# Attention scores of the last two layers from split float32r pairs, two heads in turn, with the mask added on VectorE

## The chip, the cores and the metric

The kernel runs on one core of a Trainium2 chip. The metric is device time in microseconds, the median of several runs; one further execution is profiled. The engines are TensorE (PE in the profile, its weight loads PEld), VectorE (DVE), ScalarE (ACT), GpSimd (POOL) and SyncE (SP), which issues the DMAs of the weights.

## The reference

Four layers over 256 tokens of width 1024. The first two (an mLSTM and differential attention layer, a convolution and mixture-of-experts layer) aren't touched. The last two are alike; what they compute, cut to the attention:

```
u = x * (1 + scale) + shift;  h = u @ w_in             # q, k, v of three attentions, gates
dsa: 4 heads of 64, one shared k and v; each query sees its 64 best keys by an index score
fox: 6 heads of 64; s = q k^T / 8 + cum[t] - cum[s]; causal
nsa: 6 heads of 64 in 2 groups; compressed blocks (16 keys), selected keys (ks, vs), window (kw, vw)
     o = g0 * o_cmp + g1 * o_slc + g2 * o_win          # with 256 tokens slc and win are causal
p = softmax(s with mask);  o = p @ v
y = (concat(dsa, fox, nsa) * silu(gate)) @ w_out;  x = layer_norm(ALPHA * x + (1 + gate2) * y)
```

## The kernel before

All tokens fit in two blocks of 128 (`tb`). Weights come in chunks of 1 MB over SP's queue (`Stream`, L164) and are split into a float32r part `hi` by ScalarE (L98) and a rest `lo` by VectorE or, for each third half chunk, GpSimd (L99); a product is then three float32r matmuls (`mm3`, L92 to L94). The instructions of each engine are put in order ahead of time by a planner that knows costs, so matmuls of projections stand between those of attention heads.

Each of the last two layers (`Hybrid`) runs in the order of `run`: `p_dsa`, `p_nsa` and `p_cmp` project queries, keys and values (`tok` gives tokens on partitions, tile `ht`; `feat` gives features on partitions, tile `hf`). `rope` rotates (L1477 to L1481), and `to_feat` transposes on TensorE into the one `hx` bank (L1490) and copies out by `copy`, on ScalarE and VectorE in turn (L1448, L1450). `dsa_select` finds each query's 64 best keys on VectorE (L1743 to L1753) and leaves a bfloat16 mask `sel`. Then come the heads: `nsa` (12 calls of `attn` a layer), `p_fox`, `dsa` (4), `nsa_cmp`, two `p_gates`, `fox` (6), two more `p_gates`, `gated`, and `out`.

`attn` does one head in one PSUM bank (tag `at`, five of them). For each token block it adds the mask by a bfloat16 matmul with the identity (L1703), then the float32 scores (L1704; 64 rows, 128 or 256 columns; a float32 matmul shows as two passes, each with a weight load), and for `fox` the decay by a float32r matmul over `cum` (L1707). VectorE takes the maximum (L1709), ScalarE the exponential and its sum (L1711), TensorE transposes the three blocks (L1714), `copy` brings them to SBUF, and three matmuls multiply by v (L1717 to L1719); VectorE scales (L1720 to L1723). Queries, keys and gates: `dqT`, `dkT`, `fqT`, `fkT`, `nrT`, `ksT`, `kwT`, in float32, where head h lies on partitions 0 to 63 if h is even and 64 to 127 if it is odd. `nrT`, `ksT`, `kwT` and `vs` lie in `hgt`, the tile of the gates, and are shown under that name.

Of the kernel before, what the change touches and what calls it, by code (L numbers as in the profile page):

```python
# [21 lines left out]
T = 256  # L22
# [1369 lines left out]
class HybConst:  # L1392


    def __init__(self, e, I, sb):
# [20 lines left out]
        self.causal = (e.neg_ge, e.neg_ge)  # L1416
# [6 lines left out]
class Hybrid:  # L1423
    def __init__(self, e, st, U, I, l, K, mix, sb, wk, ps):
# [3 lines left out]
        t = lambda n, *s, dt=F32: sb.tile([128, *s], dt, name=n)  # L1428
        self.mix = mix
        self.dqT, self.dkT, self.dv = t("hdqT", 2, T), t("hdkT", T), t("hdv", 2, 64)  # L1430
        self.iqT, self.ikT, self.iw = t("hiqT", 2, T), t("hikT", T), t("hiw", 2, 8)
        self.fkT, self.fv = t("hfkT", 3, T), t("hfv", 2, 384)
        self.fqT, self.nqT, self.vw = t("hfqT", 3, T), t("hnqT", 3, T), t("hvw", 2, 128)

        g = t("hgt", 8 * T)
        self.gt = g.rearrange("p (b n) -> p b n", b=2)
        v = lambda i, n, m: g[:, T * i:T * (i + n)].rearrange("p (a t) -> p a t", t=m)
        self.nrT, self.ksT, self.kwT, self.vs = v(0, 3, T), v(3, 2, T), v(5, 2, T), v(7, 1, 128)
# [44 lines left out]
    def to_feat(self, x, out):  # L1483

        e = self.e
        n = out.shape[1]
        p = self.bank("hx", "hx").rearrange("p (a t) -> p a t", a=2)
        for i in range(n):
            for tb in range(2):
                e.nc.tensor.transpose(p[:, i, 128 * tb:128 * tb + 128], x[:, tb, 128 * i:128 * i + 128], e.ident)  # L1490
        self.copy(out, p[:, :n, :])
# [11 lines left out]
    def p_dsa(self, bf):  # L1503
# [12 lines left out]
        self.to_feat(a, self.dkT[:, None, :])  # L1516
# [42 lines left out]
    def p_nsa_q(self, p, j, n):  # L1559
# [4 lines left out]
        self.to_feat(a, self.nrT[:, j:j + n // 128, :])  # L1564

    def p_fox(self):
        e, nc = self.e, self.e.nc
        for i in range(3):
            w = self.st.next()
            for f in range(2):  # L1570
                p = self.feat(w, f)
                j = 2 * i + f
                if j < 3:
                    nc.scalar.activation(self.fqT[:, j, :], p, AF.Copy, scale=0.125)
                else:
                    self.copy(self.fkT[:, j - 3, :], p)
# [58 lines left out]
    def p_nsa_kv(self):  # L1635
        nc = self.e.nc
        for kT, v in ((self.ksT, self.vs), (self.kwT, self.vw)):
# [5 lines left out]
            self.to_feat(a[:, :, 0:128], kT[:, 0:1, :])  # L1643
            self.to_feat(a[:, :, 64:192], kT[:, 1:2, :])
            nc.gpsimd.tensor_copy(v, b[:, :, 128:256])

    def p_gates(self, i):
# [3 lines left out]
        t = self.gt[:, :, 256 * i:256 * i + 256]  # L1651
# [3 lines left out]
    def gated(self, mT, i):  # L1655
# [4 lines left out]
        nc.vector.scalar_tensor_tensor(m, m, 0.5, self.gt[:, :, cs], op0=OP.mult, op1=OP.mult)  # L1660
# [4 lines left out]
        hi, lo = (x[:, 2 * i:2 * i + 2, :] for x in mT)  # L1665
# [3 lines left out]
    def run(self, bf, pe, mT, later):  # L1669
# [4 lines left out]
        self.nsa(range(3))  # L1674
        self.cmp()
        self.nsa(range(3, 6))
# [5 lines left out]
        self.fox((4, 5, 0, 1, 2, 3))  # L1682
        for i in OUT[2:]:
            self.p_gates(i)
        for i in OUT:
            self.gated(mT, i)


    def attn(self, qT, kT, v, masks, out, extra=None, gate=None):
# [5 lines left out]
        s = self.bank("as", "at")  # L1695
        o = s[:, 384:512].rearrange("p (b d) -> p b d", b=2)
        z = wk.tile([128, 2], F32, tag="az", name="az", bufs=4)
        m = wk.tile([128, 2], F32, tag="am", name="am", bufs=4)
        x = wk.tile([128, 384], F32, tag="ax", name="ax", bufs=2)
        parts = [s[:, 0:128], s[:, 128:384]]  # L1700
        for tb, st in enumerate(parts):
            n = 128 * tb + 128
            nc.tensor.matmul(st[:, n - masks[tb].shape[-1]:], e.identb, masks[tb], start=True, stop=False, skip_group_check=True)  # L1703
            nc.tensor.matmul(st, qT[:, 128 * tb:128 * tb + 128], kT[:, 0:n], start=False, stop=(extra is None),  # L1704
                             skip_group_check=True)
            if extra is not None:
                nc.tensor.matmul(st, extra[0], extra[1][:, 0:n], start=False, stop=True, skip_group_check=True)  # L1707
# [594 lines left out]
```

## Time and profile before

| | us |
|---|---|
| median of 3 runs (2023.22 to 2026.17) | 2023.52 |
| profiled execution | 2031.13 |
| its span | 2029.4 |
| mean granted TensorE clock, of 1 | 0.933 |

A median is compared with a median; durations come from the profiled execution, 2031.13 us, of which 1.7 us lie outside the span.

### The profile page before, as it was taken

The numbers are of one execution on the slowest core, as the hardware profiler recorded it, in microseconds if no ns is written. First come the engines' busy times: TensorE is split into PE (matmuls) and PEld (weight loads), VectorE is DVE, ScalarE is ACT, GpSimd is POOL, SyncE is SP. The second block draws the span as 40 slices with busy tenths as digits, with TensorE's granted clock in tenths as the row PEclk, the third lists the DMA queues.
The fourth block names the chain that finished last, engine by engine and source line by source line (L and its number), as shares of the span: only waits on it lengthen the run. The fifth ranks groups of instructions, "written<-read, shape, count | busy, mean of one in ns | idle before, by whom it ended". The sixth has DMA issues, their size and how long they took to land. (4 is left out here: it accounts for less than half of the span.)

```text
span 2029.4 us, 33102 instructions
## 1 busy us (share of the span) xinstructions
PE 1873.0 (92%) x12339; PEld 1657.9 (82%) x12339; DVE 1582.0 (78%) x2239; ACT 1189.8 (59%) x1838; POOL 517.9 (26%) x460
## 2 busy tenths in 40 slices
PE   6789889699997779999999999999997899989997
PEld 3768667699976668999999999999996888878886
DVE  5887996677669758999999999999996674568455
ACT  5455564455545447777777777777776443454333
POOL 2645662533227531000000000000001523333141
PEclk8889987799998889999999999999998988988889
DMA  9845775288753128999999999999993431233120
GB/s 361 285 154 208 244 242 178 80 323 308 250 208 127 50 83 322 366 342 338 346 365 351 333 354 358 342 342 355 355 355 115 135 105 63 89 130 111 65 72 21
DMA packets 132462, 468.41 MB, mean 231 GB/s; under 512 B 14994, under 2 KB 16274, under 8 KB 132292
## 3 DMA queue, kind: packets, MB, share of 16 engines
q1 hardware_dynamic: 131008, 464.38, 64.2%
q8 instruction: 99, 1.62, 0.3%
q10 hardware_dynamic: 1172, 1.65, 0.2%
q14 instruction: 71, 0.58, 0.1%
q0 software_dynamic: 112, 0.17, 0.1%
HBM read 465.10 MB, written 1.05 MB: 230 GB/s over the span
## 5 line engine op out<-in xcount | busy, mean ns | idle before, releaser
L99 DVE TENSOR_TENSOR lo<-raw,hi 128x1024 fp32r<-128x1024 f32 x678 | 858.1, 1280 | 134.9 <-ACT hi L98 112.3
L98 ACT CAST hi<-raw 128x1024 fp32r<-128x1024 f32 x718 | 747.1, 1050 | 300.4 <-PE ph L94 92.8
L93 PE MATMUL ph<-lo,gh 128*128 128x256 f32 x1408 | 397.0, 282 | 3.6 <-DVE lo L99 1.8
L94 PE MATMUL ph<-hi,gl 128*128 128x256 f32 x1408 | 396.7, 282 | 0.0
L92 PE MATMUL ph<-hi,gh 128*128 128x256 f32 x1408 | 394.0, 280 | 0.0
L93 PEld LDWEIGHTS ph<-lo,gh 128*128 128x128 f32 x1408 | 264.6, 188 | 12.6 <-DVE lo L99 6.9
L94 PEld LDWEIGHTS ph<-hi,gl 128*128 128x128 f32 x1408 | 264.8, 188 | 3.4
L92 PEld LDWEIGHTS ph<-hi,gh 128*128 128x128 f32 x1408 | 264.8, 188 | 2.8
L343 POOL TENSOR_TENSOR adac<-adac,raw 128x512 f32<-128x512 f32 x112 | 194.0, 1757 | 180.1 <-ACT raw L341 109.0
L1597 POOL MEMSET kv<- 64x2 f32 x4 | 0.4, 97 | 791.8 <-DVE lo L99 775.1
L99 POOL TENSOR_TENSOR lo<-raw,hi 128x1024 fp32r<-128x1024 f32 (+1 forms) x40 | 97.5, 2446 | 186.9 <-ACT hi L98 178.5
L93 PE MATMUL pe<-lo,hhi 128*128 128x512 f32 x352 | 138.0, 393 | 0.0
L92 PE MATMUL pe<-hi,hhi 128*128 128x512 f32 x352 | 137.2, 397 | 0.5 <-ACT hhi L98 0.5
L94 PE MATMUL pe<-hi,hlo 128*128 128x512 f32 x352 | 125.8, 392 | 0.0
L92 PE MATMUL ht<-hi,Hh 128*128 128x256 f32 (+1 forms) x384 | 117.8, 307 | 0.6 <-ACT u L459 0.6
L93 PE MATMUL ht<-lo,Hh 128*128 128x256 f32 (+1 forms) x384 | 116.0, 302 | 0.0
L94 PE MATMUL ht<-hi,Hl 128*128 128x256 f32 (+1 forms) x384 | 115.8, 302 | 0.0
L92 PE MATMUL ph<-Fh,hi 128*128 128x256 f32 x352 | 101.5, 290 | 11.4 <-DVE h L980 8.8
L93 PE MATMUL ph<-Fl,hi 128*128 128x256 f32 x352 | 101.4, 289 | 0.0
L94 PE MATMUL ph<-Fh,lo 128*128 128x256 f32 x352 | 100.2, 287 | 0.0
L92 PEld LDWEIGHTS ht<-hi,Hh 128*128 128x128 f32 x384 | 79.6, 207 | 2.3 <-ACT u L459 1.4
L1083 POOL TENSOR_TENSOR cyp<-cyp,ctp 128x256 f32<-128x256 f32 x83 | 72.4, 883 | 34.8 <-ACT ctp L1082 31.2
(592 smaller groups left out, 4124.3 us busy)
## 6 DMA issues: line engine op xcount, KB each, us to landing
raw<-in_l_moe_w SPq DMA_DIRECT2D x528, 512.0 KB, 5.3
raw<-in_l_mod_w SPq DMA_DIRECT2D x96, 512.0 KB, 5.4
raw<-in_l_ffn_w SPq DMA_DIRECT2D x66, 512.0 KB, 4.9
raw<-in_w_in SPq DMA_DIRECT2D x60, 512.0 KB, 3.5
raw<-in_w_ada SPq DMA_DIRECT2D x32, 512.0 KB, 5.4
raw<-in_l_w_in SPq DMA_DIRECT2D x28, 512.0 KB, 5.6
raw<-in_l_conv_pw_w SPq DMA_DIRECT2D x24, 512.0 KB, 4.3
raw<-in_w_ada SPq DMA_DIRECT2D x32, 256.0 KB, 3.7
```

The source lines that it names most:

```text
L92: mm(out, a[0], b[0], start=start, stop=False, **kw)
L93: mm(out, a[0], b[1], start=False, stop=False, **kw)
L94: return mm(out, a[1], b[0], start=False, stop=stop, **kw)
L98: nc.scalar.copy(hi, src)
L99: (lo_eng or nc.vector).tensor_tensor(lo, src, f32(hi), op=OP.subtract)
L343: nc.gpsimd.tensor_tensor(a[:, 1, i:i + 512], a[:, 1, i:i + 512], y[:, i:i + 512], op=OP.add)
L1083: nc.gpsimd.tensor_tensor(yp, yp, t, op=OP.add)
L1597: nc.gpsimd.memset(kv[64:128, :, T - 1:T], 0.0)
```

## The change

In the last two layers queries and keys of `dsa`, `fox` and the selected and window parts of `nsa` are kept as float32r pairs, `hi` and `lo`: `to_feat` splits what it transposes (ScalarE writes `hi`, VectorE subtracts for `lo`) where it copied before, and `p_fox` likewise. Scores are the three products hi hi, hi lo, lo hi. `attn` takes two heads, an even and an odd one, in a bank each, and issues their matmuls in turn. The mask matmul goes; VectorE adds the mask to the scores, writes the negated sum to SBUF and keeps its minimum, in one instruction, and the exponential reads SBUF with scale -1. `ksT` and `kwT` are transposed in one bank instead of two copies each. Tiles share memory in another way: the split output `HT` of `gated` holds `ksT`, `kwT`, `dqT` and part of `nrT` before, and the gates' tile holds `iqT`, `ikT`, `nqT`, `vs` and `vw`. The buffers `ax`, `apT` and `no` go from two to three. The products of `cum`, the transposes and the products with v stay.

```diff
-        self.causal = (e.neg_ge, e.neg_ge)
+        cz = sb.tile([128, T], BF, name="causal")
+        nc.vector.memset(cz, 0.0)
+        nc.vector.tensor_copy(cz[:, 128:T], e.neg_ge)
+        self.causal = (cz[:, 128:T], cz)
...
+        t2 = lambda n, *s: tuple(t(n + x, *s, dt=F32R) for x in "hl")
         self.mix = mix
-        self.dqT, self.dkT, self.dv = t("hdqT", 2, T), t("hdkT", T), t("hdv", 2, 64)
-        self.iqT, self.ikT, self.iw = t("hiqT", 2, T), t("hikT", T), t("hiw", 2, 8)
-        self.fkT, self.fv = t("hfkT", 3, T), t("hfv", 2, 384)
-        self.fqT, self.nqT, self.vw = t("hfqT", 3, T), t("hnqT", 3, T), t("hvw", 2, 128)
+        self.mT = t2("HT", KB, T)
+        w = lambda h, i, n: self.mT[h][:, i:i + n, :]
+        self.ksT, self.kwT = (w(0, 0, 2), w(0, 2, 2)), (w(0, 4, 2), w(0, 6, 2))
+        self.dqT, self.nrT = (w(1, 0, 2), w(1, 2, 2)), (w(1, 4, 3), t("hnrl", 3, T, dt=F32R))
+        self.dkT, self.dv = t2("hdkT", T), t("hdv", 2, 64)
+        self.fkT, self.fv = t2("hfkT", 3, T), t("hfv", 2, 384)
+        self.fqT, self.iw = t2("hfqT", 3, T), t("hiw", 2, 8)
         g = t("hgt", 8 * T)
-        self.gt = g.rearrange("p (b n) -> p b n", b=2)
+        self.gt = g.rearrange("p (i b n) -> p i b n", i=4, b=2)
         v = lambda i, n, m: g[:, T * i:T * (i + n)].rearrange("p (a t) -> p a t", t=m)
-        self.nrT, self.ksT, self.kwT, self.vs = v(0, 3, T), v(3, 2, T), v(5, 2, T), v(7, 1, 128)
+        self.iqT, self.ikT, self.nqT = v(0, 2, T), v(6, 1, T)[:, 0], v(3, 3, T)
+        self.vs, self.vw = v(7, 1, 128), v(2, 1, 128)
...
-    def to_feat(self, x, out):
+    def to_feat(self, x, out, step=128):
         e = self.e
-        n = out.shape[1]
+        n = (out[0] if isinstance(out, tuple) else out).shape[1]
         p = self.bank("hx", "hx").rearrange("p (a t) -> p a t", a=2)
         for i in range(n):
             for tb in range(2):
-                e.nc.tensor.transpose(p[:, i, 128 * tb:128 * tb + 128], x[:, tb, 128 * i:128 * i + 128], e.ident)
-        self.copy(out, p[:, :n, :])
+                e.nc.tensor.transpose(p[:, i, 128 * tb:128 * tb + 128], x[:, tb, step * i:step * i + 128], e.ident)
+        if isinstance(out, tuple):
+            e.split(*out, p[:, :n, :])
+        else:
+            self.copy(out, p[:, :n, :])
...
+                hi, lo = (x[:, j % 3, :] for x in (self.fqT if j < 3 else self.fkT))
                 if j < 3:
-                    nc.scalar.activation(self.fqT[:, j, :], p, AF.Copy, scale=0.125)
+                    nc.scalar.activation(hi, p, AF.Copy, scale=0.125)
+                    nc.vector.scalar_tensor_tensor(lo, p, 0.125, f32(hi), op0=OP.mult, op1=OP.subtract)
                 else:
-                    self.copy(self.fkT[:, j - 3, :], p)
+                    e.split(hi, lo, p)
...
-            self.to_feat(a[:, :, 0:128], kT[:, 0:1, :])
-            self.to_feat(a[:, :, 64:192], kT[:, 1:2, :])
+            self.to_feat(a, kT, 64)
...
-        self.nsa(range(3))
+        self.nsa((0,))
         self.cmp()
-        self.nsa(range(3, 6))
+        self.nsa((2, 4))
         self.p_fox()
         self.dsa()
         self.nsa_cmp()
         for i in OUT[:2]:
             self.p_gates(i)
-        self.fox((4, 5, 0, 1, 2, 3))
+        self.fox((4, 0, 2))
...
-    def attn(self, qT, kT, v, masks, out, extra=None, gate=None):
+    def attn(self, heads):
         e, nc, wk = self.e, self.e.nc, self.wk
-        s = self.bank("as", "at")
-        o = s[:, 384:512].rearrange("p (b d) -> p b d", b=2)
-        z = wk.tile([128, 2], F32, tag="az", name="az", bufs=4)
-        m = wk.tile([128, 2], F32, tag="am", name="am", bufs=4)
-        x = wk.tile([128, 384], F32, tag="ax", name="ax", bufs=2)
-        parts = [s[:, 0:128], s[:, 128:384]]
-        for tb, st in enumerate(parts):
+        ss = [self.bank("as", "at") for _ in heads]
+        cols = [slice(0, 128), slice(128, 384)]
+        for tb, cs in enumerate(cols):
             n = 128 * tb + 128
-            nc.tensor.matmul(st[:, n - masks[tb].shape[-1]:], e.identb, masks[tb], start=True, stop=False, skip_group_check=True)
-            nc.tensor.matmul(st, qT[:, 128 * tb:128 * tb + 128], kT[:, 0:n], start=False, stop=(extra is None),
-                             skip_group_check=True)
-            if extra is not None:
-                nc.tensor.matmul(st, extra[0], extra[1][:, 0:n], start=False, stop=True, skip_group_check=True)
-        for tb, st in enumerate(parts):
-            nc.vector.tensor_reduce(m[:, tb:tb + 1], st, axis=AX.X, op=OP.max, negate=True)
-        for tb, st in enumerate(parts):
-            nc.scalar.activation(x[:, 128 * tb:256 * tb + 128], st, AF.Exp, bias=m[:, tb:tb + 1], accum_out=z[:, tb:tb + 1])
-        p = s[:, :384]
-        for b in range(3):
-            nc.tensor.transpose(p[:, 128 * b:128 * b + 128], x[:, 128 * b:128 * b + 128], e.ident)
-        pT = wk.tile([128, 384], F32, tag="apT", name="apT", bufs=2)
-        self.copy(pT, p)
-        nc.tensor.matmul(o[:, 0, :], pT[:, 0:128], v(0), start=True, stop=True)
-        nc.tensor.matmul(o[:, 1, :], pT[:, 128:256], v(0), start=True, stop=False)
-        nc.tensor.matmul(o[:, 1, :], pT[:, 256:384], v(1), start=False, stop=True)
-        nc.vector.reciprocal(z, z)
-        if gate is not None:
-            nc.vector.tensor_tensor(z, z, gate, op=OP.mult)
-        nc.vector.tensor_tensor(out, o, z[:, :, None].to_broadcast([128, 2, 64]), op=OP.mult)
+            ts = slice(128 * tb, n)
+            for i, (a, b) in enumerate(((0, 0), (0, 1), (1, 0))):
+                for s, (q, k, _, _, _, extra, _) in zip(ss, heads):
+                    nc.tensor.matmul(s[:, cs], q[a][:, ts], k[b][:, 0:n], start=(i == 0), stop=(i == 2 and extra is None),
+                                     skip_group_check=True)
+            for s, (_, _, _, _, _, extra, _) in zip(ss, heads):
+                if extra is not None:
+                    nc.tensor.matmul(s[:, cs], extra[0], extra[1][:, 0:n], start=False, stop=True, skip_group_check=True)
+        for s, (_, _, v, masks, out, _, gate) in zip(ss, heads):
+            o = s[:, 384:512].rearrange("p (b d) -> p b d", b=2)
+            z = wk.tile([128, 2], F32, tag="az", name="az", bufs=4)
+            m = wk.tile([128, 2], F32, tag="am", name="am", bufs=4)
+            x = wk.tile([128, 384], F32, tag="ax", name="ax", bufs=3)
+            for tb, cs in enumerate(cols):
+                nc.vector.tensor_tensor_reduce(x[:, cs], s[:, cs], masks[tb], -1.0, 3.0e38, OP.add, OP.min, m[:, tb:tb + 1])
+            for tb, cs in enumerate(cols):
+                nc.scalar.activation(x[:, cs], x[:, cs], AF.Exp, scale=-1.0, bias=m[:, tb:tb + 1], accum_out=z[:, tb:tb + 1])
+            p = s[:, :384]
+            for b in range(3):
+                nc.tensor.transpose(p[:, 128 * b:128 * b + 128], x[:, 128 * b:128 * b + 128], e.ident)
+            pT = wk.tile([128, 384], F32, tag="apT", name="apT", bufs=3)
+            self.copy(pT, p)
+            nc.tensor.matmul(o[:, 0, :], pT[:, 0:128], v(0), start=True, stop=True)
+            nc.tensor.matmul(o[:, 1, :], pT[:, 128:256], v(0), start=True, stop=False)
+            nc.tensor.matmul(o[:, 1, :], pT[:, 256:384], v(1), start=False, stop=True)
+            nc.vector.reciprocal(z, z)
+            if gate is not None:
+                nc.vector.tensor_tensor(z, z, gate, op=OP.mult)
+            nc.vector.tensor_tensor(out, o, z[:, :, None].to_broadcast([128, 2, 64]), op=OP.mult)
...
+    def half(self, pair, h, *i):
+        r = slice(64 * (h % 2), 64 * (h % 2) + 64)
+        return tuple(x[(r, *i, slice(None))] for x in pair)
     def dsa(self):
-        for h in range(4):
-            r = slice(64 * (h % 2), 64 * (h % 2) + 64)
-            self.attn(self.dqT[r, h // 2, :], self.dkT[r, :], lambda b: self.dv[:, b, :], self.sel,
-                      self.mix[:, :, 64 * h:64 * h + 64])
+        for h0 in (0, 2):
+            self.attn([(self.half(self.dqT, h, h // 2), self.half(self.dkT, h), lambda b: self.dv[:, b, :], self.sel,
+                        self.mix[:, :, 64 * h:64 * h + 64], None, None) for h in (h0, h0 + 1)])
...
+        for h0 in heads:
+            hs = (h0, h0 + 1)
+            o = [self.mix[:, :, 640 + 64 * h:704 + 64 * h] for h in hs]
             for i, (kT, v) in enumerate(((self.ksT, self.vs), (self.kwT, self.vw))):
-                o = self.mix[:, :, 640 + 64 * h:704 + 64 * h]
-                t = self.wk.tile([128, 2, 64], F32, tag="no", name="no", bufs=2) if i else o
-                self.attn(self.nrT[r, h // 2, :], kT[r, k, :], lambda b: v[:, b, 64 * g:64 * g + 64],
-                          self.K.causal, t, gate=self.ng[:, :, 6 + 6 * i + h])
+                t = [self.wk.tile([128, 2, 64], F32, tag="no", name="no", bufs=3) for _ in hs] if i else o
+                self.attn([(self.half(self.nrT, h, h // 2), self.half(kT, h, (h // 3 + h) % 2),
+                            lambda b, h=h: v[:, b, 64 * (h // 3):64 * (h // 3) + 64], self.K.causal, t[h - h0], None,
+                            self.ng[:, :, 6 + 6 * i + h]) for h in hs])
                 if i:
-                    nc.gpsimd.tensor_tensor(o, o, t, op=OP.add)
+                    for a, b in zip(o, t):
+                        nc.gpsimd.tensor_tensor(a, a, b, op=OP.add)
```

## Rows read from the trace of the kernel before

**Rows 1.** The chain that ended last, whole span: its shares by line.

```profile
by line: PE as L1704 2.4%; PE ht L92 1.9%; PE ht L93 1.8%; PE ht L94 1.8%; PE as L1714 0.9%; PE hf L93 0.8%; PE hf L92 0.8%; PE hf L94 0.7%; PE hy L92 0.7%; PE hy L93 0.7%; PE hy L94 0.7%; PE as L1703 0.5%; DVE rb L1479 0.5%; PE as L1719 0.
```

**Rows 2.** Stretches: length, busy PE, PEld, DVE, ACT, POOL; clock, DMA share, GB/s.

```profile
1603.00:1636.00 33.00, 31.04 (x250) 28.57 (x248) 29.34 (x71) 16.11 (x26) 16.72 (x12) 1.00 0.41 134
1636.00:1766.00 130.00, 129.22 (x843) 109.19 (x841) 70.04 (x187) 50.29 (x136) 34.70 (x21) 0.86 0.24 78
...
1868.00:1993.00 125.00, 123.53 (x830) 105.73 (x830) 65.44 (x170) 47.24 (x131) 35.49 (x20) 0.89 0.18 61
```

**Rows 3.** Timeline of PE from 1670.4: start, us, engine, line, operation, tiles.

```profile
1670.50 0.23 PE L1703 MATMUL as<-neg_ge,identb 128*128 128x128 bf16 x1
1670.65 0.48 PE L1704 MATMUL as<-hgt 64*128 64x128 f32 x2
1671.07 0.23 PE L1703 MATMUL as<-neg_ge,identb 128*128 128x128 bf16 x1
1671.23 0.70 PE L1704 MATMUL as<-hgt 64*128 64x256 f32 x2
1671.86 0.23 PE L1703 MATMUL as<-neg_ge,identb 128*128 128x128 bf16 x1
...
1675.33 1.22 PE L1704 MATMUL as<-hgt 64*128 64x256 f32 x2
```

**Rows 4.** Timeline of PE's weight loads, the same block.

```profile
1671.23 0.29 PEld L1704 LDWEIGHTS as<-hgt 64*128 64x128 f32 x2
```

**Rows 5.** Timeline of PE in layer 0, around L831's scores.

```profile
141.19 1.12 PE L831 MATMUL ds<-dkT,dqT 64*128 64x512 f32 x2
142.24 0.38 PE L92 MATMUL pk<-hi,Uh 128*128 128x256 f32 x1
...
219.01 1.13 PE L831 MATMUL ds<-dkT,dqT 64*128 64x512 f32 x4
220.07 0.50 PE L92 MATMUL pf<-Uh,hi 128*128 128x512 f32 x1
```

**Rows 6.** The chain in order of time, in a projection: start, us.

```profile
1600.11 0.12 PE ht L93
```

**Rows 7.** Timeline of PE from 1732.3, the `cum` matmuls of one `fox` head.

```profile
1732.76 0.33 PE L1707 MATMUL as<-cum,idr 128*128 128x128 f32 x1
...
1733.71 0.38 PE L1707 MATMUL as<-cum,idr 128*128 128x256 f32 x1
```

**Rows 8.** Groups by line and shape from 1480: busy us, mean ns; idle before.

```profile
L98 ACT CAST hi<-raw 128x1024 fp32r<-128x1024 f32 x121 | 125.5, 1050 | 74.8 <-PE ht L94 42.8 <-issue 11.4 <-PE hf L93 9.2
L99 DVE TENSOR_TENSOR lo<-raw,hi 128x1024 fp32r<-128x1024 f32 x92 | 120.5, 1322 | 19.9 <-ACT hi L98 18.2
L1709 DVE TENSOR_REDUCE am<-as 128x1 f32<-128x256 f32 x44 | 18.2, 413 | 0.0
L1711 ACT ACTIVATION_READ_ACCUMULATOR ax<-as,am 128x1 f32 x88 | 17.6, 200 | 0.0
L1667 DVE TENSOR_TENSOR HTl<-hmt,HTh 128x512 fp32r<-128x512 f32 x8 | 5.5, 689 | 12.7 <-ACT HTh L1666 12.7
L1666 ACT CAST HTh<-hmt 128x512 fp32r<-128x512 f32 x8 | 4.7, 591 | 10.6 <-PE hmt L1664 10.6
L99 DVE TENSOR_TENSOR hlo<-hq,hhi 128x256 fp32r<-128x256 f32 x9 | 3.8, 421 | 0.6 <-ACT hhi L98 0.5
L1450 DVE COPY hgt<-hx 128x256 f32<-128x256 f32 x4 | 1.7, 417 | 0.1
L1450 DVE COPY hdqT<-hx 128x512 f32<-128x512 f32 x2 | 1.4, 684 | 0.0
```

**Rows 9.** The chain in order of time, where the attention begins.

```profile
1635.12 0.35 DVE hgt L1450
...
1636.33 0.42 PE as L1704 x2
```

**Rows 10.** The score banks' instructions, 1636 to 1766: length, PE, PEld, DVE, ACT.

```profile
1636.00:1766.00 130.00, 65.54 (x342) 41.06 (x298) 25.86 (x77) 24.66 (x99) 0.86 0.24 78
```

## What the change will do: the prediction

> **What bounds the kernel now.** I read the chain that ended last first, because only work on it can shorten the run. Its line totals [rows 1] are to be read as shares of 2029.4 us: the score matmuls of `attn` (L1704) hold 2.4%, which is 48.7 us, and the mask matmuls (L1703) 0.5%, 10.1 us. Together 58.9 us of the path is the work that this change replaces, all of it on TensorE.
>
> Next I cut the last two layers into stretches [rows 2]. In the two stretches in which the attention runs (130 and 125 us) TensorE is busy for 129.2 and 123.5 us, VectorE for 70 and 65, ScalarE for 50 and 47, and DMA moves 78 and 61 GB/s: TensorE sets the pace, and the others have half of their time free. The granted clock is 0.86 and 0.89 there, a mean of 1 and 0.5, so about 36 and 27 us (twice what is missing from 1, by the length) are spent at the lower level, 1.2 GHz. In the stretches ahead of them, where the projections are rotated, transposed and stored, VectorE is the bound: 29.3 of 33 us in the first of the two layers, and the other has the like. So work added to VectorE costs little behind the start of the attention and is paid in full ahead of it.
>
> **What a head costs TensorE.** [rows 3] shows the instructions of one head: mask, 128-column scores, mask, 256-column scores, and then the next head's mask. One head takes 1671.86 - 1670.50 = 1.36 us at full clock: 0.15 + 0.42 + 0.16 + 0.63. Forty-four heads make 59.8 us, which agrees with the chain's 58.9. The two score blocks differ by 0.21 us for 128 columns and two float32 passes, so a pass takes 0.105 us for 128 columns. What is left of 0.42 us after two such passes is 0.21: the first weight load, 0.11 (the second of the two loads starts 0.11 after the first, [rows 4]: two of 0.19 in 0.29), and 0.10 to leave the 64-row arrangement. The second load is over at 1671.52 while the first pass of that 256-column block still runs, so a later load is hidden.
>
> **The same after.** A head needs three passes for each block instead of two, so their price and their overlap decide. For the price: the two `cum` matmuls are already float32r, 0.33 us for 128 columns and 0.38 for 256 [rows 7], so 128 columns more cost 0.05 us, half of a float32 pass. In the projections a load and a 256-column float32r pass follow each other every 0.12 us [rows 6]. I take 0.12 for either block, since the load of 0.11 fills the shorter one. For the overlap: layer 0 has float32 scores of 512 columns on halves of the rows [rows 5]. Two passes on one half take 1.05 us (141.19 to 142.24); four passes on both halves, into two banks, take 1.06 us (219.01 to 220.07). Two halves run at once and cost what one costs. The new code puts the heads of a pair on opposite halves, in turn and in banks of their own, which is that case. So a pair has six double passes: 0.11 + 6 x 0.12 + 0.10 = 0.93 us where two heads took 2.72. The six pairs of `fox` leave and re-enter the 64-row arrangement once more for `cum`, 0.21 each; the `cum` matmuls themselves stay 24 in number. Twenty-two pairs: 16 x 0.93 + 6 x 1.14 = 21.7 us. Saved are 59.8 - 21.7 = 38.1, and 37.5 by the chain's 58.9.
>
> The Trainium skill, "TensorE: Matmul & The Clock Gate", section "The mechanism", says that a weight load overlaps a matmul in flight only where the row group differs. The hidden second load of [rows 4] disagrees with it on one half; what it would give is the third rival.
>
> **Work that moves to VectorE and ScalarE.** The maximum (0.41 us for 256 columns, [rows 8]) becomes an addition of the mask with a running minimum. No row shows that instruction. From below it costs what the maximum costs, since a two-input VectorE instruction on 256 columns out of a bank takes 0.42. From above it costs a second instruction for the minimum, at the 0.20 us of ScalarE's read of its sum: 88 x 0.20 = 17.6 us more of VectorE. I take the lower price, its form being nearest; at either the stretches keep VectorE below 85 of about 110 us, and it is hidden by TensorE. The exponentials read SBUF instead of the bank; I leave their time as it is. The six lower halves of the `fox` queries and keys in each layer are subtractions of 0.42 us in the same stretch, hidden likewise. If TensorE ceased to be the bound there, these would count: that is the last rival.
>
> Ahead of the attention nothing hides them. Each layer splits six results (two of 256 columns, four of 512). VectorE subtracts 2 x 0.42 + 4 x 0.69 = 3.6 us and gives up copies of about 1.9 (0.42 for 256 columns and 0.68 for 512, every second one): 1.7 more. The chain enters the attention over a copy out of the one `hx` bank, a transpose and the first scores [rows 9]; that 0.42 us copy turns into 0.59 on ScalarE and then 0.69 on VectorE, 0.9 more. And every split holds `hx` for one more queue. From below this is 1.7 us a layer. From above each of the six splits also waits for a weight cast on ScalarE and a weight subtraction on VectorE, 1.05 and 1.32 long, so 6 x 2.4 more, less what one copy's queue costs now: some 12 a layer. I take 4, nearer to the lower end because the transposes of that stretch are spread out. For two layers that is 8 us, with ends 3.4 and 24.
>
> The tiles that now share memory (`HT` with queries and keys, the gates with `iqT`, `ikT`, `nqT`, `vs`, `vw`) add waits only for instructions that stand behind the last reader in the program's order, so I cost them at nothing; were one of them early, a projection's result would wait in its bank, which the next case covers. The DMAs are the same in number, size and order; SP and POOL get nothing. The mask matmuls, the 0.15 and 0.16 above, are gone with their loads.
>
> **Sum.** -37.5 + 8 = -29.5 us. The profiled execution took 2031.1 us, 7.6 above the median of the runs; the forecast is for the median: 2023.5 - 29.5 = 1994.0 us.
>
> **Rivals.**
> *Halves that don't overlap*, because other matmuls are put between the heads of a pair or a bank comes late. Then twelve single passes: 0.11 + 12 x 0.12 + 0.10 = 1.65 us a pair, 37.6 us in all, saved 22, net 14: about 2009. For it speaks that in [rows 5] both kinds stand in one kernel; against it, that the new loop issues the heads in turn.
> *The clock stays up.* The lower level covers some 64 us of the two stretches; it falls inside the stream of [rows 3], whose last block at 1675.33 takes 1.22 us instead of 0.70, and that stream shrinks to a third. Were half of the 64 us granted at 2.4 GHz instead of 1.2, 16 us more would go: 1978. Against it: the gaps between the streams may keep it low.
> *Loads that aren't hidden on their own half*: 3 x (0.11 + 0.05) + 3 x (0.11 + 0.11) + 0.10, about 1.25 us a pair, 28.8 us in all, saved 30.6, net 23: 2001. Against it stands [rows 4]. This is the case that the skill's page above names.
> *The projections pay it all back*: `hx` is one bank, and if each of the twelve splits costs 2.5 us the 30 us are gone: 2024, no change. A cast of 1.05 and a subtraction of 1.32 in front of every one of them [rows 8] would nearly make it.
> *The softmax becomes the bound, and the kernel slower.* A pair holds two of the five `at` banks through scores, minimum, exponentials, transposes and products, so two pairs are in flight where five heads were. On the score banks VectorE and ScalarE need 25.9 and 24.7 us for 11 pairs [rows 10], 2.4 and 2.2 us each, longer than TensorE's 0.93 for the scores. If TensorE has no projection at hand in the order, it waits, and from 1.35 us a pair on (29.5 / 22) nothing is won; at 2 us it is 44 - 29.5 = 14.5 us slower, 2038. For it: the bank count. Against it: TensorE has some 196 us of other work in these stretches, and sat idle for only 2 us there.
>
> **How the numbers follow.** Forecast 0.60 (its own range 1982 to 2004), no overlap 0.12, clock 0.10, loads 0.05, paid back 0.05, softmax 0.08. The low end adds the clock's 16 us and takes the low price of the splits: 2023.5 - 37.5 - 16 + 3.4, about 1973. The high end is no overlap (22 saved) with 12 us for the splits: 2014. Outside are the last two cases and the tails, just under 0.2. A difference of 0.2%, 4 us, is about what can be told from no change. Faster takes all of the first four but 0.01: 0.86; same 0.06; slower 0.08.
>
> **What would show it.** The score line should have 44 x 6 passes, in pairs that start within 0.02 us, some 0.9 to 1.0 us a pair, and about 22 us of the chain instead of 59; the mask line should be gone. The attention stretches should be about 110 and 106 us long with TensorE still without idle time, and VectorE's minimum at 0.3 and 0.42 us. The stretches ahead of them should be 2 to 6 us longer, with splits out of `hx` in the chain. I am wrong if the passes of a pair stand one behind the other, if TensorE waits for exponentials or minima inside the attention, or if the projections take over 10 us more a layer.

## The result and the profile after

The changed kernel takes 1997.56 us, the median of 4 runs (1990.54 to 2003.04), where the kernel before takes 2024.85 in the same session: 0.9858 of it, with a 95% interval of 0.9818 to 0.9898. That is 27.3 us less; the forecast was 29.5 less. The profiled execution took 2003.04 us, the longest of the four, with a span of 2001.3.

The chain that ended last, whole span, its shares by line, to be laid beside [rows 1]:

```profile
by line: PE as L1719 1.6%; PE ht L92 1.5%; PE ht L94 1.5%; PE ht L93 1.5%; issue 1.0%; PE as L1736 0.9%; PE hf L92 0.7%; PE hf L93 0.7%; DVE lo L99 0.7%; PE hf L94 0.7%; DVE rb L1490 0.7%; PE hy L94 0.7%; PE hy L92 0.7%; PE hy L93 0.7%; PE 
```

The scores, now L1719, hold 1.6% of 2001.3 us, 32 us, where scores and mask held 58.9. The mask line is gone.

The two attention stretches, from the first score to the first transpose of `gated`, first of the kernel before and then of the changed one (columns as in [rows 2]):

```profile
1636.10:1764.60 128.50, 128.50 (x838) 108.75 (x837) 68.54 (x184) 49.06 (x134) 34.60 (x21) 0.85 0.24 79
1864.20:1990.90 126.70, 124.48 (x833) 105.88 (x832) 67.90 (x176) 47.97 (x132) 36.81 (x21) 0.89 0.19 63
```

```profile
1635.80:1750.00 114.20, 109.51 (x832) 100.45 (x833) 71.10 (x226) 48.50 (x132) 34.74 (x19) 0.89 0.25 82
1847.80:1962.70 114.90, 112.22 (x829) 103.57 (x829) 66.85 (x227) 49.10 (x133) 36.47 (x21) 0.88 0.20 70
```

They are 14.3 and 11.8 us shorter, 26.1 in all, which is nearly the whole of the 28.1 us between the two spans. (Another 3.0 lie ahead of the last two layers, whose first projection starts at 1565.2 in place of 1568.2, in code that is the same.) TensorE now stands idle for 4.7 and 2.7 us of the two stretches (length less busy time), where it was 0 and 2.2. The clock is 0.89 and 0.88, where it was 0.85 and 0.89.

The stretches ahead of them, from the first projection of the layer to its first score, first of the kernel before and then of the changed one:

```profile
1568.20:1636.10 67.90, 59.96 (x451) 56.51 (x451) 47.48 (x95) 33.06 (x52) 36.73 (x26) 0.92 0.38 121
1800.10:1864.20 64.10, 62.77 (x472) 59.43 (x473) 53.70 (x114) 32.96 (x52) 30.29 (x22) 0.91 0.41 141
```

```profile
1565.20:1635.80 70.60, 60.89 (x454) 57.16 (x454) 51.48 (x104) 35.65 (x58) 37.92 (x27) 0.89 0.41 128
1786.20:1847.80 61.60, 60.04 (x475) 56.44 (x475) 53.86 (x113) 33.73 (x54) 30.78 (x22) 0.97 0.43 147
```

The timeline of TensorE shows what became of [rows 3]: a pair kept together, and one head of a pair alone.

```profile
1658.40 0.45 PE L1719 MATMUL as<-HTh,HTl 64*128 64x128 f32 x4
1658.68 0.28 PE L1719 MATMUL as<-HTh,hnrl 64*128 64x128 f32 x2
1658.79 0.46 PE L1719 MATMUL as<-HTh,HTl 64*128 64x256 f32 x4
1659.08 0.29 PE L1719 MATMUL as<-HTh,hnrl 64*128 64x256 f32 x2
1659.30 0.39 PE L94 MATMUL hf<-Hh,lo 128*128 128x256 f32 x1
...
1664.57 0.43 PE L1719 MATMUL as<-HTh,HTl 64*128 64x128 f32 x2
1664.84 0.27 PE L1719 MATMUL as<-HTh,hnrl 64*128 64x128 f32 x1
1664.96 0.45 PE L1719 MATMUL as<-HTh,HTl 64*128 64x256 f32 x2
1665.24 0.28 PE L1719 MATMUL as<-HTh,hnrl 64*128 64x256 f32 x1
1665.45 0.38 PE L94 MATMUL hf<-Hh,lo 128*128 128x256 f32 x1
```

Twelve passes of two heads take 1659.30 - 1658.40 = 0.90 us, and six passes of one head take 0.88. So the halves do overlap fully where the two heads stand side by side. But the planner often moves one head's passes away from the other's: of the 264 passes in the trace 126 start within 25 ns of another and 138 start alone.

The groups by line and shape, from 1480, that answer to [rows 8]:

```profile
L1731 DVE CUSTOM_DVE_ANT_0 ax<-as,causal 128x256 f32<-128x256 f32 x36 | 15.1, 419 | 0.0
L1731 DVE CUSTOM_DVE_ANT_0 ax<-as,causal 128x128 f32<-128x128 f32 x36 | 10.3, 286 | 13.7 <-PE as L1723 9.2 <-PE as L1719 4.0 <-PE as L1736 0.5
L1731 DVE DVE_READ_ACCUMULATOR2_ANT am<- 128x1 f32 x88 | 7.2, 82 | 0.0
L99 DVE TENSOR_TENSOR HTh<-hx,HTh 128x512 fp32r<-128x512 f32 x4 | 2.7, 682 | 0.1
L98 ACT CAST HTl<-hx 128x512 fp32r<-128x512 f32 x4 | 2.4, 588 | 1.3 <-PE hx L1501 1.3
```

Mask and minimum cost 0.42 us for 256 columns and 0.29 for 128, as the maximum did, and a small read of 82 ns behind each; the splits have the forecast's durations.

The waits of TensorE in the two attention stretches (for what, us in all, times, longest), the two longest of the first and the longest of the second:

```profile
PE cs L1838 <- DVE cx L1835: 4.0, 1, 4.0
PE as L1719 <- ACT HTh L98: 1.8, 1, 1.8
PE bg L384 <- ACT hgtb L385: 1.5, 1, 1.5
```

The second is the first score of the layer, which waits for its split. The first is new. The chain in order of time (start, us, what), where the compressed attention of the first of the two layers ends:

```profile
1707.21 1.21 DVE lo L99
...
1709.62 2.51 DVE xs L1675
1712.13 2.27 DVE cmx L1832
...
1714.89 2.52 DVE cx L1835
...
1717.46 0.66 PE cs L1838 x2
1718.12 0.94 PE as L1719 x5
```

TensorE waits 4.0 us for `cx` here, behind two long VectorE instructions (`xs`, the gate product, 2.51 us here and 0.68 before, and `cmx`). In the kernel before, the same work ran from 1726.6 to 1734.0 beside projection matmuls (`ht`), and TensorE waited for none of it.

### The profile page after: what moved, and what is told of

It is laid out like the page before. It is cut to its first block, busy times and chain, and to the rows that moved or that the text cites. A ratio compares the mean times of both kernels' runs of the same rounds, so it can differ in the third digit from the quotient of the medians.

```text
span 2001.3 us, 33220 instructions
## 1 busy us (share of the span) xinstructions
PE 1834.0 (92%) x12339; PEld 1636.7 (82%) x12339; DVE 1590.6 (79%) x2343; ACT 1192.3 (60%) x1844; POOL 520.9 (26%) x460
## 3 DMA queue, kind: packets, MB, share of 16 engines
q8 instruction: 99, 1.62, 0.3%
## 5 line engine op out<-in xcount | busy, mean ns | idle before, releaser
L92 PEld LDWEIGHTS ph<-Fh,hi 128*128 128x128 f32 x352 | 68.2, 195 | 14.5 <-DVE h L980 9.1
```

The source lines that it names most:

```text
L92: mm(out, a[0], b[0], start=start, stop=False, **kw)
```

## The experiments

Each ran for five rounds beside the kernel before. The table puts them side by side. "Scores" is the time from the start of each score, mask or `cum` matmul to the start of TensorE's next instruction, without the time in which TensorE then stood idle, added up over both attention stretches of the profiled execution. "Idle" is TensorE's idle time there. "Rest" is what every other instruction takes; it is nearly the same work in all of them, so it shows what the clock does. "Clock" is the granted clock of the two stretches.

| kernel | median us | of before, 95% | scores | idle | rest | clock |
|---|---|---|---|---|---|---|
| before | 2023.5 | 1 | 70.3 | 2.2 | 182.7 | 0.85, 0.89 |
| changed | 1997.6 | 0.9858 (0.9818 to 0.9898) | 39.7 | 7.4 | 182.2 | 0.89, 0.88 |
| e1_single | 2016.2 | 0.9943 (0.9925 to 0.9961) | 50.5 | 6.9 | 185.3 | 0.86, 0.89 |
| e2_f32_pairs | 1991.3 | 0.9825 (0.9799 to 0.9850) | 42.3 | 8.3 | 172.9 | 0.93, 0.95 |
| e3_mask_only | 1988.6 | 0.9818 (0.9794 to 0.9841) | 41.1 | 7.2 | 171.0 | 0.92, 0.98 |
| e4_kept_pairs | 1987.1 | 0.9806 (0.9783 to 0.9829) | 31.1 | 8.1 | 177.0 | 0.89, 0.94 |
| e5_f32_kept | 1981.6 | 0.9791 (0.9768 to 0.9814) | 34.8 | 4.0 | 177.5 | 0.84, 0.95 |
| e6_mask_on_tensore | 2015.6 | 0.9951 (0.9933 to 0.9968) | 59.1 | 11.8 | 179.2 | 0.87, 0.84 |
| e7_masks_first | 2005.6 | 0.9904 (0.9878 to 0.9931) | 55.2 | 5.8 | 167.7 | 0.94, 0.98 |
| e8_split_two_passes | 1990.1 | 0.9829 (0.9806 to 0.9852) | 40.6 | 2.8 | 170.4 | 0.94, 0.97 |
| e9_one_pass | 1974.2 | 0.9732 (0.9706 to 0.9759) | 25.5 | 5.0 | 176.9 | 0.89, 0.92 |
| c1_single_cum_last | 1979.7 | 0.9774 (0.9750 to 0.9798) | 35.6 | 4.8 | 171.0 | 0.94, 0.98 |
| c2_kept_cum_last | 1985.5 | 0.9789 (0.9762 to 0.9816) | 33.5 | 4.5 | 178.2 | 0.90, 0.88 |

The last four columns stand for one execution each. In the changed kernel, e1, e6, e9 and c2 it is the longest that was measured (e9's took 1987.97 us, 13.7 above its median), and that of the kernel before is 7.6 above its own.

My theory was that the gain is TensorE's time on scores and masks, and that the planner's order keeps half of the pairs from overlapping. The rivals were that pairs win nothing, that the split is what pays, and that the softmax sets the pace.

**e1_single: the changed kernel, heads one at a time.**

```diff
-        for h0 in (0, 2):
+        for h0 in range(4):
...
-                        self.mix[:, :, 64 * h:64 * h + 64], None, None) for h in (h0, h0 + 1)])
+                        self.mix[:, :, 64 * h:64 * h + 64], None, None) for h in (h0,)])
```

The same in `nsa` and `fox`, with the heads in the order of before.

> The changed kernel with its heads one at a time again (queries and keys still split, three float32r passes a block, mask on VectorE, heads in the order of before). Theory A (the halves of the rows overlap, as far as the order of the instructions leaves the two heads of a pair side by side): a head alone costs TensorE 0.11 + 6 x 0.12 + 0.10 = 0.93 us, and the twelve with cum 0.21 more, 43.4 us for 44 heads, against 34.9 us that the score and cum lines hold in the changed kernel; so 8 us slower than the changed kernel, 0.990 of before, and no passes that start within 25 ns of each other. Theory B (the pairing wins nothing, and the loss of two score banks to a pair costs as much): equal to the changed kernel, 0.985 to 0.987 of before, or faster.

It lost 18.6 us of the changed kernel's gain by medians, twice what theory A gave, and theory B falls. The score columns differ by 10.8 us, near the 8 worked out; the rest is 3.1 longer. (38 of its passes still start beside another, of heads that happen to be neighbours.)

**e3_mask_only: before, and only the mask moved to VectorE.**

```diff
-            nc.tensor.matmul(st[:, n - masks[tb].shape[-1]:], e.identb, masks[tb], start=True, stop=False, skip_group_check=True)
-            nc.tensor.matmul(st, qT[:, 128 * tb:128 * tb + 128], kT[:, 0:n], start=False, stop=(extra is None),
+            nc.tensor.matmul(st, qT[:, 128 * tb:128 * tb + 128], kT[:, 0:n], start=True, stop=(extra is None),
...
-            nc.vector.tensor_reduce(m[:, tb:tb + 1], st, axis=AX.X, op=OP.max, negate=True)
+            nc.vector.tensor_tensor_reduce(x[:, 128 * tb:256 * tb + 128], st, masks[tb], -1.0, 3.0e38, OP.add, OP.min, m[:, tb:tb + 1])
...
-            nc.scalar.activation(x[:, 128 * tb:256 * tb + 128], st, AF.Exp, bias=m[:, tb:tb + 1], accum_out=z[:, tb:tb + 1])
+            xs = x[:, 128 * tb:256 * tb + 128]
+            nc.scalar.activation(xs, xs, AF.Exp, scale=-1.0, bias=m[:, tb:tb + 1], accum_out=z[:, tb:tb + 1])
```

> The kernel before with one part of the change alone: VectorE adds the mask and takes the minimum, the mask matmuls are gone; float32 queries and keys, heads one at a time. Theory A: the two blocks of a head now follow each other, so a head costs 0.11 + 0.21 + 0.42 + 0.10 = 0.84 us where it cost 1.36, and the twelve with cum 0.21 more: 39.5 us against 59.8, 20 us saved, 0.990 of before (2003 to 2005 us). So most of the whole change's 27 us comes from the mask alone. Theory C (the split and the pairs are what pays): the masks give back only the 10.1 us of their own line on the chain, 0.995 of before, or less where VectorE's additions are late.

This one part gives at least the whole change's gain: 0.9818. Theory C falls, and theory A's 0.990 was exceeded. The timeline of its TensorE shows a head:

```profile
1659.38 1.69 PE L1706 MATMUL as<-hgt 64*128 64x128 f32 x12
1661.00 0.39 PE L93 MATMUL hf<-Hl,hi 128*128 128x256 f32 x1
...
1662.14 0.92 PE L1706 MATMUL as<-hgt 64*128 64x128 f32 x4
1662.99 0.38 PE L92 MATMUL hf<-Hh,hi 128*128 128x256 f32 x1
```

One head takes 0.85 us, as worked out, and was 1.36 in [rows 3]. Three heads in a row take 1.62, less than three times that, because neighbours on opposite halves overlap without being paired. It saved more than the 20 us expected: the score column is 29.2 us shorter and the rest 11.7, at a clock of 0.92 and 0.98, less 5.0 of idle time. Its windows:

```profile
1629.10:1742.60 113.50, 107.56 (x794) 94.53 (x794) 69.03 (x228) 50.07 (x134) 35.04 (x21) 0.92 0.27 90
1840.20:1946.10 105.90, 104.69 (x789) 91.77 (x788) 67.30 (x220) 48.97 (x132) 34.64 (x21) 0.98 0.22 76
```

**e2_f32_pairs: mask on VectorE and pairs, with float32 scores and no split.** Its `attn` is the changed one with one matmul of `q` and `k` in place of the three.

> Float32 queries and keys as in the kernel before, with no splits; mask on VectorE and two heads in turn as in the changed kernel. Theory A (what pays is that the masks leave TensorE and the halves overlap; the split is not needed, since two float32 passes of 0.105 and 0.21 us take as long as three float32r passes of 0.12): a pair costs 0.11 + 2 x 0.105 + 2 x 0.21 + 0.10 = 0.84 us, about what the split ones take, and the 3 to 8 us of splits ahead of the attention are gone: 0.981 to 0.985 of before, 0 to 8 us faster than the changed kernel. Theory C (the split is what pays: float32 passes do not overlap, or the shorter float32r ones are what shrinks the score line): a pair costs 1.47 us or more, the score line stays near 40 us, and it is slower than the changed kernel by over 5 us, 0.989 or more of before.

It is as fast as theory A said, and for the time the split isn't needed. But pairs by themselves won nothing over single heads (1991.3 against 1988.6): only 56 of its 176 passes start beside another, 48 with single heads.

**e4_kept_pairs: the changed kernel, with each score pass held behind the one before.**

```diff
-                for s, (q, k, _, _, _, extra, _) in zip(ss, heads):
-                    nc.tensor.matmul(s[:, cs], q[a][:, ts], k[b][:, 0:n], start=(i == 0), stop=(i == 2 and extra is None),
...
+                for s, (q, k, _, _, _, extra, _) in list(zip(ss, heads))[::-1]:
+                    with ExitStack() as c:
+                        if last is not None:
+                            c.enter_context(e.tc.issue_after(last.ins))
+                        last = nc.tensor.matmul(s[:, cs], q[a][:, ts], k[b][:, 0:n], start=(i == 0), stop=(i == 2 and extra is None),
...
```

> The changed kernel with each score pass held behind the one before it in the order, so that the heads of every pair stay in turn. Theory A: all 132 double passes overlap, the score and cum lines fall from 34.9 to about 22 us, and the kernel is up to 13 us faster than the changed one, 0.979 to 0.983 of before. Theory D (the softmax sets the pace of a pair: VectorE and ScalarE need 2.4 and 2.2 us for it and two of the five score banks are held): TensorE waits for what the scores gave up, the kernel is equal to the changed one or slower, 0.986 to 0.992, with waits for exponentials or minima at the transposes.

(The two heads of a pair are also issued in the other order.) 224 of its 264 passes have a partner, the score column is 8.6 us shorter than the changed kernel's, the rest 5.2, and the median 10.4 us lower. Theory D falls: waits for exponentials come to 1.6 us in both stretches.

**e5_f32_kept: the same holding on the float32 pairs of e2.**

> Float32 queries and keys, mask on VectorE, heads in pairs, and each score pass held behind the one before it in the order, so that the heads of every pair stay in turn (the float32 pairs that were not held took 41.3 us on the score line, as much as single heads, 38.0, since only 56 of their 176 instructions started beside a partner). Theory A (halves overlap, the order keeps them apart): a pair costs 0.84 us, the score line falls to about 20 us, and the kernel takes 0.970 to 0.977 of before, 10 to 20 us less than the pairs that were not held. Theory D (with the mask gone the scores are no longer what TensorE is short of: what it gains here it waits for at the transposes or spends at the lower clock): 0.979 to 0.984, as the float32 pairs and single heads.

0.9791 lies at the low end of theory D's band; theory A's is missed, though the interval (from 0.9768) reaches into it. The score column fell by 7.5 us from e2's, with 118 of 176 passes beside a partner, but the rest is 4.6 longer, at a clock of 0.84 in the first stretch.

**e6_mask_on_tensore: the changed kernel with the mask matmuls of before.**

```diff
+            for s, (_, _, _, masks, _, _, _) in zip(ss, heads):
+                w = masks[tb].shape[-1]
+                nc.tensor.matmul(s[:, cs.stop - w:cs.stop], e.identb, masks[tb], start=True, stop=False, skip_group_check=True)
             for i, (a, b) in enumerate(((0, 0), (0, 1), (1, 0))):
...
-                nc.vector.tensor_tensor_reduce(x[:, cs], s[:, cs], masks[tb], -1.0, 3.0e38, OP.add, OP.min, m[:, tb:tb + 1])
+                nc.vector.tensor_reduce(m[:, tb:tb + 1], s[:, cs], axis=AX.X, op=OP.max, negate=True)
...
```

> The other half of the change alone: split queries and keys, three float32r passes, two heads in turn, but the mask as in the kernel before, by matmuls on TensorE, with the maximum on VectorE and the exponentials out of the bank. Theory E (the mask that leaves TensorE carries the whole gain: alone it gave 0.9818 of before, and the split gives part of that back): 0.996 to 1.004 of before, no gain or a loss. Theory C (split and turns carry at least the 27 us less the 10.1 us of the mask line): 0.990 to 0.993.

Split and turns alone gain 8 to 10 us, just outside theory E's band, into which the interval reaches, and 4 us from theory C's. Taking the mask away from this version is worth 18 us more.

**e7_masks_first: before, with both masks ahead of both score blocks.**

```diff
         for tb, st in enumerate(parts):
             n = 128 * tb + 128
-            nc.tensor.matmul(st[:, n - masks[tb].shape[-1]:], e.identb, masks[tb], start=True, stop=False, skip_group_check=True)
+            last = nc.tensor.matmul(st[:, n - masks[tb].shape[-1]:], e.identb, masks[tb], start=(tb == 0), stop=False,
+                                    skip_group_check=True)
+        for tb, st in enumerate(parts):
+            n = 128 * tb + 128
+            with e.tc.issue_after(last.ins):
+                last = nc.tensor.matmul(st, qT[:, 128 * tb:128 * tb + 128], kT[:, 0:n], start=False, stop=(extra is None),
...
```

> The kernel before with one thing changed: both mask matmuls of a head stand ahead of both score blocks, which follow each other; nothing leaves TensorE. Theory F (what a mask costs is above all the way out of the 64-row arrangement and back between the two blocks, 0.21 us a head, beside 0.31 for the two mask matmuls): 44 x 0.21 = 9 us less, up to 14 where masks move into idle time, 0.993 to 0.996 of before. Theory G (the mask's price is its matmuls and the lower clock that they bring, not where they stand): 0.998 to 1.001.

Nothing left TensorE, and it is 18 us faster. The timeline of its TensorE:

```profile
1667.46 0.29 PE L1703 MATMUL as<-neg_ge,identb 128*128 128x128 bf16 x2
1667.67 0.92 PE L1708 MATMUL as<-hgt 64*128 64x128 f32 x4
1668.52 0.29 PE L1703 MATMUL as<-neg_ge,identb 128*128 128x128 bf16 x2
```

A head takes 1668.52 - 1667.46 = 1.06 us, 0.30 less than [rows 3]: both masks 0.21, both blocks 0.85. 44 x 0.30 is 13.2 of the 15.1 us by which the score column fell. The rest fell by 15.0 as well, at a clock of 0.94 and 0.98, and 3.6 us of idle time came. So theory F is right on where the price lies, and its size was exceeded by what came with the clock.

The Trainium skill, "TensorEngine Tiling (Array Packing)", section "Key Properties", says that a change of the tiling mode drains TensorE. These runs fit that: between the same matmuls, one way out of the 64-row arrangement and back costs 0.30 us a head.

**e8_split_two_passes: e1 with two-pass float32 scores of the upper halves.**

```diff
-            for i, (a, b) in enumerate(((0, 0), (0, 1), (1, 0))):
+            for i in range(1):
...
-                    nc.tensor.matmul(s[:, cs], q[a][:, ts], k[b][:, 0:n], start=(i == 0), stop=(i == 2 and extra is None),
+                    nc.tensor.matmul(s[:, cs], f32(q[0][:, ts]), f32(k[0][:, 0:n]), start=True, stop=(extra is None),
```

> Heads one at a time and split queries and keys as in the run of single heads (0.9943 of before), but the scores are two-pass float32 matmuls of the upper halves alone: the lower halves are computed and not read, so the scores lack their lower part. It has the split work of that run and the TensorE work of the run with the mask alone (0.9818). Theory H (the 25 us between those two runs come from the third pass and the lower clock that comes with it): 0.983 to 0.987, the 4 to 5 us of splits ahead of the attention slower than the mask alone. Theory I (they come from the splits: their ScalarE and VectorE work, and the one bank that they hold): 0.990 to 0.995.

Theory H, at its edge. The split work by itself costs 1.5 us (against e3, within the error). Three float32r passes in place of two float32 ones cost 26 us (e1 against this); in the profiled executions 9.9 of it stand in the score column, 4.1 in idle time and 14.9 in the rest, at the lower clock.

**e9_one_pass: e1 with the first pass alone** (`enumerate(((0, 0),))`).

> Split queries and keys, heads one at a time, mask on VectorE, but only the first of the three float32r passes (upper half by upper half): the two passes with lower halves are left out, so the scores lack them. TensorE's score work is the least of all runs, 0.11 + 0.12 + 0.10 and 0.21 for each of the 24 cum: some 20 us, against 35.8 us measured for two float32 passes of the same upper halves (0.9829 of before) and 44.1 us for three float32r passes (0.9943). Theory J (the third pass costs by its work, and the lower clock follows from more work): 0.974 to 0.979, 8 to 16 us less than the two float32 passes. Theory K (float32r passes on half of the rows bring the lower clock, whatever their number: the mean granted clock of the two attention stretches was 0.86 and 0.89 with them and 0.94 and 0.97 with float32 passes): the clock stays below 0.91 in both stretches, and the time is 0.981 or more.

The windows of the two attention stretches, of e8 and then of e9:

```profile
1638.70:1744.10 105.40, 105.39 (x788) 94.14 (x789) 70.19 (x227) 48.55 (x131) 36.20 (x19) 0.94 0.27 88
1841.30:1949.70 108.40, 105.56 (x785) 93.08 (x785) 71.03 (x228) 49.09 (x133) 35.06 (x21) 0.97 0.22 74
```

```profile
1641.60:1744.30 102.70, 101.95 (x739) 92.44 (x740) 69.62 (x225) 48.15 (x131) 36.51 (x19) 0.89 0.28 91
1842.90:1947.60 104.70, 100.48 (x741) 92.26 (x741) 72.73 (x228) 49.03 (x133) 35.92 (x21) 0.92 0.24 77
```

The time is just under theory J's band, and the interval reaches into it. In the profiled execution the clock is 0.89 and 0.92, lower than with the two float32 passes of e8, and of the 15.1 us saved in the score column 6.5 go back into the rest and 2.2 into idle time. But that execution is the longest of its six, at 0.940 over the whole kernel; four others had 0.948 to 0.950, where e8's profiled one, at its median, had 0.949, and by medians e9 saves all of 15.9 us against e8. Theory K falls by the time; its clock was met in the first stretch of that one execution alone. What sets the clock stays open.

**c1_single_cum_last and c2_kept_cum_last: candidates.** In e3 and e5, `cum` goes behind both score blocks, and the blocks are held together. In c1:

```diff
+        last = None
+        for x_ in (0, 1)[:1 if extra is None else 2]:
+            for tb, st in enumerate(parts):
+                n = 128 * tb + 128
+                q, k = (extra[0], extra[1]) if x_ else (qT[:, 128 * tb:128 * tb + 128], kT)
+                with ExitStack() as c:
+                    if last is not None:
+                        c.enter_context(e.tc.issue_after(last.ins))
+                    last = nc.tensor.matmul(st, q, k[:, 0:n], start=(tb == 0 and not x_), stop=(x_ == 1 or extra is None),
...
```

> A candidate for the fastest: the mask alone on VectorE, float32, heads one at a time (0.9818 of before), with both score blocks of a head side by side in the order and, for the twelve heads that have them, both cum matmuls behind them, so that the 64-row arrangement is left once and not twice: 12 x 0.21 = 2.5 us less, 0.979 to 0.982. If what is left of the scores no longer counts on TensorE: 0.981 to 0.984.

> The same edit on the held float32 pairs (0.9791 of before): both cum matmuls of a pair behind all its score blocks, 6 x 0.21 = 1.3 us less and heads kept in turn across the two blocks: 0.976 to 0.980. If the waits at the start of the attention and the clock of 0.84 in that stretch decide, no better than 0.979.

c1 takes 1979.7 us, 8.9 less than the mask alone and about 18 less than the changed kernel: heads one at a time, no split, its score column 5.5 us below e3's. It has the lowest median of the kernels that compute the whole scores (e8 and e9 leave the lower halves out). That is somewhat more than the 2.5 us worked out, and its interval (to 0.9798) reaches into the band expected. c2 gains nothing over e5; its 0.9789 lies in the band forecast and also just at the limit of the other theory, so it decides nothing.

## Why the prediction came out right, point by point

**The total** was right: 27.3 us less against 29.5, inside the range. That it came so near is luck: two terms were off by 6 to 12 us, in opposite directions.

**The price of a head and of a pair** was right at full clock: 0.90 us for a pair against 0.93. That loads are hidden on their own half was right too: a head alone takes 0.88 us, and with loads that are not hidden it would take 1.25. The rule of the Trainium skill, "TensorE: Matmul & The Clock Gate", section "The mechanism", that the forecast weighed is not borne out for these shapes.

**Overlap of all pairs** was the step that failed: "six double passes" in 0.93 us for each of 22 pairs. Fewer than half of the passes had a partner. With `cum` the score column is 39.7 us; with the pairs held (e4) it is 31.1, and the kernel 10 us faster. The first rival, halves that don't overlap because other matmuls are put between the heads, was half of the truth. The forecast argued from the loop's order in the code, and the planner decides the order on TensorE.

**What was saved all the same** is 25.4 us in place of 37.5: the scores, masks and `cum` went from 70.3 to 39.7 us, 30.6 less, and TensorE's idle time rose by 5.2, where the forecast had none. So the stretches are 114.2 and 114.9 us long in place of the 110 and 106 forecast. The 70.3 is at the clock that they really had; the forecast's 59.8 and 58.9 were figures at full clock and of the chain, without `cum`, so the start of the sum was low by some 6 us (70.3 less 4.9 of `cum`, against 59.8) and hid a part of what the order cost.

**The splits ahead of the attention** were taken at +8 us, with ends 3.4 and 24. From the first projection to the first score it went from 67.9 to 70.6 us in one layer and from 64.1 to 61.6 in the other (at a clock of 0.97 after 0.91), and e8 against e3 prices all of the split work at 1.5 us: the lower end, and less. The forecast took VectorE for the bound there, but the row that it read has TensorE busy for 31.0 of the 33 us and VectorE for 29.3 [rows 2]. The 6 to 8 us by which this term was too high made up for over half of what the attention fell short.

**Mask and minimum on VectorE** came at the lower price (0.42 us), and the 82 ns reads stay hidden: VectorE is busy for 71.1 and 66.9 of some 114 us. **The softmax** did not become the bound. What did become late is the compressed attention, 4.0 us in one layer, which the forecast did not name; e3 waits 2.3 us and e6 3.7 and 3.5 for the same tile, so it is not of the split or of the moved mask alone.

**The clock** rose little in the changed kernel (0.89 and 0.88), so that rival didn't come; e3, e7, e8 and c1 show that it can (0.92 to 0.98), and there the rest, work that wasn't touched, is 12 to 15 us shorter.

**What the forecast did not see** is that the parts pull against each other. The mask's departure alone is worth some 36 us. The split then takes back some 28 (e1 against e3). For the two blocks of a head, of 128 and 256 columns, six float32r passes of 0.12 us, 0.72, are no less than two float32 passes of 0.105 and two of 0.21, 0.63; but 44 x 0.09 explains only 4 us of the 28. In the profiled executions the scores are 9.4 us longer and the rest 14.3, at the lower clock, whose cause stays open. Turns give back about 19. Both prices of a pass stood in [rows 3] and [rows 6], but the forecast set old against new as a whole and never part against part.

## What to carry to other kernels

Price each part of a change alone, with the old version of the others: here one of three carried the gain and another, added to it, was a loss. Look on TensorE for instructions that change the arrangement of its rows between two that share one; putting them side by side paid without removing any work. Where two heads should overlap, their order on the engine has to be held, and counted in the trace.

## What the runs showed of the hardware that was not expected

- Mask matmuls between the score blocks of a head cost 0.21 us for the two, and 0.30 us more for the way out of the 64-row arrangement and back (1.36 against 1.06 us), and with them came a lower clock: 0.85 and 0.89 against 0.94 and 0.98 in the attention stretches, and over the whole kernel 0.936 to 0.940 in the eleven executions beside e7 against 0.942 to 0.954 in its six.
- Single heads with three float32r passes had a lower granted clock than with two float32 ones: 0.86 and 0.89 in the attention stretches of e1 against 0.92 to 0.98 in those of e3, e8 and c1, each in one profiled execution, and over the whole kernel 0.932 to 0.941 in the twelve executions of e1 against 0.942 to 0.952 in the sixteen of the others. With one float32r pass (e9) it was 0.940 to 0.950 over the whole kernel, so it is not shown that float32r as such brings it. Held pairs had 0.84 to 0.95 in the stretches with either.
- The running minimum of VectorE's two-input operation shows as an instruction of its own of 82 ns.
